# Sample-token side work in pairs: scores, values and state products of two samples issued together

## Chip, cores and metric

The kernel runs on one core of a Trainium2 chip. The metric is the device time of one launch in microseconds (us); lower is better. Before the change three runs gave 1600.12, 1600.78 and 1602.69 us; their median, 1600.78 us, is the time to compare with.

## What is computed

A decoder trunk of two layers runs one step for a prompt of 256 tokens and for 8 samples of 4 tokens each; both share the weights, so 288 token columns go past every weight tile. A layer is a half-step feed-forward (SwiGLU), a mixer with three branches (causal pooling, a Mamba-2 scan, cross-attention into 256 memory tokens), and a second half-step feed-forward. Three parts of the mixer belong to the samples alone, because every sample has its own cache. In the reference they are these lines, with L = 4 tokens for each of 8 samples:

```python
# cross-attention: k and v are the sample's cached keys and values (256, 4 heads, 128)
s = einsum('blhd,bmhd->bhlm', q, k) * 128 ** -0.5
w = softmax(s, axis=-1)
y = einsum('bhlm,bmhd->blhd', w, v)
# scan: h0 is the sample's cached state (16 heads, 64, 128), for one chunk of 4 tokens
y_off  = einsum('tgn,ghpn->tghp', cm, h0) * exp(acum)
h_last = h0 * exp(acum[-1]) + einsum('sgn,sghp->ghpn', bm, xdt * to_end)
```

The new state `h_last` of every sample is an output, 512 KB each; the cached keys, values and states are inputs of 512 KB per sample and layer.

## The kernel before

**The stream.** All weights lie in one packed array of 128x128 float32 tiles, in the order in which TensorE needs them. `Stream` (line 107) brings them in slabs of 8 tiles (SyncE issues the load `raw`, 512 KB), splits each slab into a high part `whi` (ScalarE, line 139) and a low part `wlo` (VectorE, or GpSimd while `pool_share` is set, line 148), and `mm3` (line 282) then makes three products of 288 columns for each tile: 24 matmuls per slab.

**Ticks and steps.** When `take()` (line 152) reaches a new slab, it calls `tick(s)` (line 162): load slab s+5, split, then `step()`, then split slab s+3 (high) and s+2 (low). `step()` (line 168) goes through the list of side work that is under way, in the order in which it was started, and runs one stage of each, that is, the Python generator up to its next `yield`. An item started with `delay` d sits out d steps first. So the place of a side instruction is fixed by the step in which its stage runs and by its item's place in the list; each engine runs its own instructions strictly in that program order. `W.finish()` runs the rest of an item at once.

**The mixer's steps.** `mixer()` (line 564) goes through groups of products: the query group `q` (4 slabs), 16 groups `xbc` (one slab each), 4 groups `u`, 8 groups `z`, then gates `g0`, `g2`, `g1` interleaved with the branch products `b0`, `b2`, `b1`, then `o`. During `xbc` every group starts a `conv` (line 587: VectorE and ScalarE work on 315 columns) and the low parts are made by GpSimd. "q-step n" is below the n-th step after the start of the `q` group, "u-step n" the n-th after the start of the first `u` group (u-step 0 is q-step 20).

**Side work of the samples.** For a sample b:
- `scores(b)` (line 1015) is started with delay 3 + b of the `q` group. It loads `kb`, and three steps later issues 4 matmuls of 32 output columns each (8 instructions in the trace, since a float32 product takes two) into the bank `ps_s`.
- `values(b)` (line 1039) has delay 17 + b: load `vb`, three steps later 8 matmuls (16 instructions) into `ps_av`. `load_prompt_kv` (line 1064) takes two buffers of the same pool at q-step 24.
- `sample_state(b)` (line 781) is started with delay 8 + 2b of the `u` group. Stage 0 loads the state `hb`; stage 1 lets GpSimd make `bm`, the sample's masked copy of B; stage 2 issues the `ps_yo` products (8 instructions of 32 columns), lets GpSimd multiply `hb` by its decay, and issues 4 `ps_up` matmuls that read `bm`; stage 3 lets VectorE add `ps_up` to `hb` (two instructions); stage 4 stores `hb`. Sample 7 also ends the sum `ps_yo` (its copy `ysb`, two transposes, `yoff`).

`sample_y` (line 902) and `group_norm` (line 915) come behind with delays 28 and 30 and end before the `b1` products. The caches share the pool `k4` of 5 buffers; `bm` lives in the pool `t2` of 5; PSUM has 7 rotating banks and one (`sum_bank`) for the sums `ps_s`, `ps_av`, `ps_yo` in turn. `pool_mix` (line 955) of a `u` group has GpSimd sums `pw`, then VectorE's `pd`, then the product `ps_pool`.

Of the kernel before, what the change touches and what calls it, by code (L numbers as in the profile page):

```python
# [20 lines left out]
NM = 256  # L21
# [23 lines left out]
def group_order(tiles, cuts):  # L45
    """Weight tiles (tile, k) of a group of products: all tiles up to each cut of k in turn."""
    for a, b in zip((0,) + cuts[:-1], cuts):
        for t in tiles:
            for k in range(a, b):
                yield t, k  # L50
# [56 lines left out]
class Stream:  # L107
    """Runs the packed weight tiles past TensorE, each split into two float32r parts.

    Every SLAB tiles make a tick: the split of a later slab is issued, then one stage  # L110
    of every piece of side work that is under way."""

# [8 lines left out]
    def parts(self, n):  # L121
        """The first slab comes in two halves, so that the products can begin."""
        k = 2 if n == 0 else 1
        return [slice(j * SLAB * P // k, (j + 1) * SLAB * P // k) for j in range(k)]
# [64 lines left out]
def trunk_kernel(ctx, tc, wpack, xT, memT, vecs, consts, wdt, wpool, hpool, hconv, h0T, kT, vC,  # L189
# [9 lines left out]
    ep = ctx.enter_context(tc.tile_pool(name="ep", bufs=2))  # L199
    t2 = ctx.enter_context(tc.tile_pool(name="t2", bufs=5))  # L200
    sp = ctx.enter_context(tc.tile_pool(name="sp", bufs=1))
# [7 lines left out]
    def tmp(name, cols=T, parts=P, dt=F32):  # L209
        return tp.tile([P, 384], dt, tag="t", name=name)[:parts, :cols]  # L210

# [9 lines left out]
    def blocks(name):  # L221
        """Two tiles of zeros for block_fill()."""
        us = [unit(f"{name}{j}") for j in range(2)]
        for u in us:
            G.memset(u, 0.0)
        return us

    def block_fill(us, srcs, copy):
        """Block b of 32 columns, of each of the four slices, gets the slice's samples with all but sample b zero."""
        for u, src in zip(us, srcs):  # L230
            copy(u.rearrange("p a (b s) -> p a b s", b=DB)[:, :, :, 0:DL], src.rearrange("p a (b t) -> p a b t", b=DB))
# [58 lines left out]
    def products(tiles, cuts, xs):  # L290
        """One PSUM bank per tile: W[:, cols].T @ x."""
        ps = [bank("ps") for _ in tiles]
        for j, k in group_order(range(len(tiles)), cuts):
            mm3(ps[j][:, :T], W.take(), chunk(xs[0], k), chunk(xs[1], k), k == 0, k == cuts[-1] - 1)
        return ps
# [9 lines left out]
    def rstd_cols(accs, starts, width, name):  # L305
        """1 / sqrt(mean + eps) of the column sums of accs, tokens on partitions: [128, len(accs) * len(starts)]."""
        n = len(accs) * len(starts)
        ps = bank("ps_" + name)
        for a, acc in enumerate(accs):
            for j, s in enumerate(starts):  # L310
                k = a * len(starts) + j
                mm(ps[:, k:k + 1], acc[:, s:s + P], ones[:, 0:1])
        v = sp.tile([P, 12], F32, tag="rs_v", name="rs_v", bufs=2)[:, :n]
        ts(v, ps[:, :n], 1.0 / width, ALU.mult, EPS, ALU.add)
        r = sp.tile([P, 12], F32, tag="rs_r", name="rs_r", bufs=2)[:, :n]
        act(r, v, AF.Sqrt)
        V.reciprocal(out=r, in_=r)
        stt(v, v, -0.5, r, ALU.mult, ALU.mult)
        tt(v, v, r, ALU.mult)
        stt(r, v, 1.5, r, ALU.add, ALU.mult)  # L320
        return r

    def rstd_rows(r, t, sums, width):
        """r = 1 / sqrt(sums / width + eps), elementwise; stages."""
        yield
# [10 lines left out]
    def spread(r):  # L336
        """out[p, t] = r of token t, for every partition p; r holds tokens 0.., 128.., 160.. by column."""
        ps = bank("ps_spread")
# [5 lines left out]
    class Norm:  # L344
        """Collects sum(x^2) chunk by chunk and splits x * gain for the products."""

# [22 lines left out]
    class Final:  # L369
        """The last norm: x * gain in place, then its scale and the output."""  # L370

# [38 lines left out]

# [1 line left out]
    mem = [unit(f"mem{j}") for j in range(KC // 2)]  # L412
# [112 lines left out]

# [1 line left out]
    def ffn(i, which, cur, nxt):  # L527
# [34 lines left out]

# [1 line left out]
    def mixer(i, cur, nxt):  # L564
# [65 lines left out]
        def dt_work(ps_dt):  # L630
# [18 lines left out]
            yield  # L649
            # log1p(e) = 2 atanh(e / (2 + e))  # L650
            ts(s, e, 2.0, ALU.add)
# [11 lines left out]
            yield  # L663
            # cumulative sums, heads on partitions and tokens on partitions; sums to the end of the group
            ph = bank("ps_nac")
# [115 lines left out]
        def sample_state(b):  # L781
            hb = k4.tile([P, D], F32, tag="k4", name="hb")
            nc.sync.dma_start(out=hb, in_=h0T[i, b])
            yield
            bm = wide("bm", 96, 512, F32R)
            tt(bm, Bst.bitcast(F32), con[:96, K_BM + b:K_BM + b + 1].to_broadcast([96, 512]), ALU.mult, G)
            yield
            if b == 0:
                yo.append(sum_bank("ps_yo"))
            for g in range(4):  # L790
                mm(yo[0][TS * g:TS * g + TS, :256], block(cm, g, b), hb[:, g * 256:(g + 1) * 256], b == 0, b == DB - 1)
            h3 = hb.rearrange("p (h d) -> p h d", h=H)
            tt(h3, h3, Ee[:, b, :].unsqueeze(2).to_broadcast([P, H, 64]), ALU.mult, G)
            pu = [bank("ps_up0"), bank("ps_up1")]
            for g in range(4):
                mm(pu[g // 2][:, (g % 2) * 256:(g % 2 + 1) * 256], bm[:, g * P:(g + 1) * P],
                   xst[g // 2][:, (g % 2) * 256:(g % 2 + 1) * 256])
            yield
            if b == DB - 1:
                ysb = wide("ysb", P, 256)  # L800
                act(ysb, yo[0][:, :256], AF.Copy)
            for q in range(2):
                tt(hb[:, q * 512:(q + 1) * 512], hb[:, q * 512:(q + 1) * 512], pu[q], ALU.add)
            yield
            nc.sync.dma_start(out=o_ssm_s[i, b], in_=hb)
            if b == DB - 1:
                pt = bank("ps_yot")
# [6 lines left out]
        def heads4(g):  # L814
            """Four heads of the prompt's scan: two pairs of heads, one group of B and C."""
            hs = slice(4 * g, 4 * g + 4)
# [169 lines left out]
        def softmax(ps, n):  # L986
            """Rows of ps [128, n, 256] (scores) to weights; stages."""
            sc = P ** -0.5
# [26 lines left out]
        def scores(b):  # L1015
            kb = k4.tile([P, 4, NM], F32, tag="k4", name="kb")
            nc.sync.dma_start(out=kb, in_=kT[i, b])
            yield
            yield
            yield  # L1020
            if b == 0:
                sc_.append(sum_bank("ps_s"))
            for h in range(4):
                mm(sc_[0][TS * h:TS * h + TS, :NM], block(qm, h, b), kb[:, h, :], b == 0, b == DB - 1)

# [13 lines left out]
        def values(b):  # L1039
            vb = k4.tile([P, 2, 512], F32, tag="k4", name="vb")  # L1040
            nc.sync.dma_start(out=vb, in_=vC[i, b])
            yield
            yield
            yield
            if b == 0:
                av.append(sum_bank("ps_av"))
            for m in range(2):
                for h in range(4):
                    mm(av[0][TS * h:TS * h + TS, :P], block(pm[m], h, b), vb[:, m, h * P:(h + 1) * P],
                       b == 0 and m == 0, b == DB - 1 and m == 1)  # L1050
            if b == DB - 1:
                yield
# [88 lines left out]
        for kind, cs, tiles, cuts in mixer_groups():  # L1141
            c = cs[0]
            # side work that this group's products need, or that can begin here
            if kind == "q":
                items["qm"] = W.start(q_blocks(), 2)
                items["sc"] = [W.start(scores(b), 3 + b) for b in range(DB)]
                items["sw"] = W.start(sample_weights(), 15)
                items["kv"] = W.start(load_prompt_kv(), 24)
                items["va"] = [W.start(values(b), 17 + b) for b in range(DB)]
                items["ph"] = [W.start(prompt_head(h), 27 + 5 * h // 2) for h in range(4)]  # L1150
                ym.extend(unit(f"ym{j}") for j in range(2))
            if kind == "u" and c == 0:
                W.pool_share = 0
                items["xss"] = W.start(xss_work(), 3)
                items["ss"] = [W.start(sample_state(b), 8 + 2 * b) for b in range(DB)]
                items["pairs"] = [W.start(heads4(g), 4 + 4 * g) for g in range(4)]
                items["yo"] = W.start(sample_y(), 28)
                items["gn"] = W.start(group_norm(), 30)
            if kind == "z" and c == 0:
# [182 lines left out]
```

## Time and profile before

| what | value |
|---|---|
| median of 3 runs | 1600.78 us (1600.12 to 1602.69) |
| span of the profiled execution, first to last instruction (the page gives no other time of it) | 1597.1 us |
| TensorE busy | 1558.0 us (98%), 11792 matmuls |
| VectorE / ScalarE / GpSimd busy | 1066.3 / 804.0 / 302.9 us |
| DMA moved | 278.00 MB, mean 174 GB/s |
| loads of `kb`, `vb`, `hb`; stores of `hb` | 16 each, 512 KB each |

PE is TensorE, DVE VectorE, ACT ScalarE, POOL GpSimd, SPq the queue of SyncE that issues all DMAs. Matmuls overlap in the array, so the trace shows the start of each; the cost of a batch is best read from the distance between starts. The page's chain of work follows what ended last backwards. [...]

### The profile page before, as it was taken

What the parts mean: (1) busy time and instruction counts of PE and PEld (TensorE: products, weight loads), DVE (VectorE), ACT (ScalarE), POOL (GpSimd) and SP (SyncE); (2) the same over time, 40 slices, a digit from 0 to 9 for tenths busy, and PEclk for the clock granted to TensorE, in tenths of its full rate; (3) what the DMA queues carried; (4) which work ended last, traced back from release to release, by engine and by line L of the source; (5) the groups of instructions that cost most, each with busy time, mean ns of one, the idle gap of its engine ahead of it and who ended that gap; (6) DMA issues with size and microseconds to landing.
All of it is one profiled execution on the core that took longest, in us unless ns stands there. A gap on an engine that the chain in (4) does not pass through costs nothing.

```text
span 1597.1 us, 29305 instructions
## 1 busy us (share of the span) xinstructions
PE 1558.0 (98%) x11792; PEld 1502.7 (94%) x11792; DVE 1066.3 (67%) x1598; ACT 804.0 (50%) x1231; POOL 302.9 (19%) x368
## 2 busy tenths in 40 slices
PE   7999999988999999999999999999999999999997
PEld 6899999887889999999999999988888999999997
DVE  6765645788777867656456665588778786766643
ACT  7444434465565546444445444456557454644442
POOL 3000001368233102000000000046823320200001
PEclk9999999999999999999999999999999999999999
DMA  6744444546465454444444444554655545444452
GB/s 244 230 167 166 164 165 171 196 147 233 168 212 193 147 173 167 162 165 166 165 166 160 171 161 169 178 185 151 238 170 188 203 159 169 158 168 167 159 171 70
DMA packets 81287, 278.00 MB, mean 174 GB/s; under 512 B 9088, under 2 KB 14336, under 8 KB 81152
## 3 DMA queue, kind: packets, MB, share of 16 engines
q1 hardware_dynamic: 81152, 276.14, 50.2%
q8 instruction: 92, 1.51, 0.4%
q14 instruction: 43, 0.35, 0.1%
HBM read 262.39 MB, written 13.71 MB: 173 GB/s over the span
## 4 chain that ended last, share of the span: by engine, by line
PE 87%; DVE 8%; ACT 2%; DMA 1%; POOL 1%; issue 1%; SPq 0%; DVEq 0%; ACTq 0%; POOLq 0%
PE ps L249 61%; PE pd L249 18%; DVE cacc L246 4%; PE ps_y L249 2%; PE ps_v L249 1%; PE ps_k L249 1%; ACT L252 1%; DMA raw<-wpack 1%; PE ps_up L249 1%; DVE wlo L148 1%; DVE cbuf L237 1%; ACT cacc L252 1%; PE ps_yo L249 1%; ACT whi L139 1%; PE ps_sp L249 0%
## 5 line engine op out<-in xcount | busy, mean ns | idle before, releaser
L148 DVE TENSOR_TENSOR wlo<-raw,whi 128x1024 fp32r<-128x1024 f32 (+1 forms) x409 | 517.8, 1267 | 266.8 <-ACT hidh L252 99.9
L139 ACT ACTIVATE whi<-raw 128x1024 fp32r<-128x1024 f32 (+1 forms) x441 | 463.7, 1054 | 329.3 <-PE ps L249 153.2
L249 PE MATMUL ps<-n1h,whi 128*128 128x288 f32 x896 | 274.4, 306 | 5.4 <-DVE Bst L237 5.4
L249 PE MATMUL ps<-n1h,wlo 128*128 128x288 f32 x896 | 266.9, 298 | 4.8 <-POOL wlo L148 4.8
L249 PE MATMUL ps<-n1l,whi 128*128 128x288 f32 x896 | 266.3, 297 | 0.0
L249 PE MATMUL ps<-n2h,whi 128*128 128x288 f32 x704 | 208.8, 297 | 0.0
L249 PE MATMUL ps<-n0h,whi 128*128 128x288 f32 x704 | 208.6, 296 | 0.0
L249 PE MATMUL pd<-hidh,whi 128*128 128x288 f32 x704 | 208.4, 296 | 0.0
L249 PE MATMUL ps<-n0l,whi 128*128 128x288 f32 x704 | 207.7, 295 | 0.0
L249 PE MATMUL pd<-hidl,whi 128*128 128x288 f32 x704 | 207.7, 295 | 0.0
L249 PE MATMUL ps<-n2l,whi 128*128 128x288 f32 x704 | 207.7, 295 | 0.0
L249 PE MATMUL ps<-n2h,wlo 128*128 128x288 f32 x704 | 207.0, 294 | 0.0
L249 PE MATMUL ps<-n0h,wlo 128*128 128x288 f32 x704 | 207.0, 294 | 0.0
L249 PE MATMUL pd<-hidh,wlo 128*128 128x288 f32 x704 | 207.0, 294 | 0.0
L237 POOL TENSOR_TENSOR acc<-acc,sqr 128x288 f32<-128x288 f32 x42 | 44.7, 1064 | 786.9 <-ACT sqr L252 785.9
L249 PEld LDWEIGHTS ps<-n1h,whi 128*128 128x128 f32 x896 | 170.3, 190 | 16.1 <-DVE Bst L237 5.8
L249 PEld LDWEIGHTS ps<-n1h,wlo 128*128 128x128 f32 x896 | 170.4, 190 | 7.3 <-POOL wlo L148 6.9
L249 PEld LDWEIGHTS ps<-n1l,whi 128*128 128x128 f32 x896 | 170.5, 190 | 0.7
L249 PEld LDWEIGHTS ps<-n0h,wlo 128*128 128x128 f32 x704 | 132.6, 188 | 0.0
L249 PEld LDWEIGHTS pd<-hidh,wlo 128*128 128x128 f32 x704 | 132.6, 188 | 0.0
L249 PEld LDWEIGHTS ps<-n2h,wlo 128*128 128x128 f32 x704 | 132.6, 188 | 0.0
L249 PEld LDWEIGHTS ps<-n2l,whi 128*128 128x128 f32 x704 | 132.1, 188 | 0.1
(297 smaller groups left out, 2877.5 us busy)
## 6 DMA issues: line engine op xcount, KB each, us to landing
raw<-wpack SPq DMA_DIRECT2D x439, 512.0 KB, 3.3
kb<-kT SPq DMA_DIRECT2D x16, 512.0 KB, 5.1
vb<-vC SPq DMA_DIRECT2D x16, 512.0 KB, 4.6
hb<-h0T SPq DMA_DIRECT2D x16, 512.0 KB, 5.8
o_ssm_s<-hb SPq DMA_DIRECT2D x16, 512.0 KB, 5.0
x<-xT SPq DMA_DIRECT2D x4, 288.0 KB, 4.1
o_y<-x SPq DMA_DIRECT2D x8, 144.0 KB, 1.8
mem<-memT SPq DMA_DIRECT2D x4, 256.0 KB, 4.6
```

The lines of the kernel that those rows point to most:

```text
L139: nc.scalar.activation(out=hi[:, a], in_=self.loaded[self.n_hi][:, a], func=AF.Copy)
L148: eng.tensor_tensor(out=lo[:, a], in0=raw[:, a], in1=self.his[n][:, a].bitcast(F32), op=ALU.subtract)
L237: (eng or V).tensor_tensor(out=out, in0=a, in1=b, op=op)
L246: V.scalar_tensor_tensor(out=out, in0=a, scalar=s, in1=b, op0=op0, op1=op1)
L249: PE.matmul(out, lhsT=lhsT, rhs=rhs, start=start, stop=stop)
L252: A.activation(out=out, in_=a, func=func, **kw)
```

## The change

Scores, values and states are handled for samples b and b+1 by one item. The pair's loads are issued in two successive steps. `scores` and `values` then issue the products of both samples in one stage. `sample_state` makes the mask of b, issues the `ps_yo` products of both samples in one stage with the `ps_up` products of b, and makes the mask of b+1 behind the first decay; the `ps_up` products of b+1 come one step later. The delays are 6 + 5p for pair p, and `sample_y` and `group_norm` start one step later. The pool `t2` gets a sixth buffer, and the buffers of `tp` go from 384 to 320 columns. The other edits blank comments.

```diff
-    t2 = ctx.enter_context(tc.tile_pool(name="t2", bufs=5))
+    t2 = ctx.enter_context(tc.tile_pool(name="t2", bufs=6))
-        return tp.tile([P, 384], dt, tag="t", name=name)[:parts, :cols]
+        return tp.tile([P, 320], dt, tag="t", name=name)[:parts, :cols]
...
         def sample_state(b):
+            def masked(c):
+                bm = wide("bm", 96, 512, F32R)
+                tt(bm, Bst.bitcast(F32), con[:96, K_BM + c:K_BM + c + 1].to_broadcast([96, 512]), ALU.mult, G)
+                return bm
+            hbs = []
+            for c in (b, b + 1):
+                hbs.append(k4.tile([P, D], F32, tag="k4", name="hb"))
+                nc.sync.dma_start(out=hbs[-1], in_=h0T[i, c])
+                yield
+            bm = masked(b)
             yield
             if b == 0:
                 yo.append(sum_bank("ps_yo"))
+            for c, hb in zip((b, b + 1), hbs):
+                for g in range(4):
+                    mm(yo[0][TS * g:TS * g + TS, :256], block(cm, g, c), hb[:, g * 256:(g + 1) * 256], c == 0, c == DB - 1)
+            for c, hb in zip((b, b + 1), hbs):
+                h3 = hb.rearrange("p (h d) -> p h d", h=H)
+                tt(h3, h3, Ee[:, c, :].unsqueeze(2).to_broadcast([P, H, 64]), ALU.mult, G)
+                pu = [bank("ps_up0"), bank("ps_up1")]
+                for g in range(4):
+                    mm(pu[g // 2][:, (g % 2) * 256:(g % 2 + 1) * 256], bm[:, g * P:(g + 1) * P],
+                       xst[g // 2][:, (g % 2) * 256:(g % 2 + 1) * 256])
+                if c == b:
+                    bm = masked(c + 1)
+                yield
+                if c == DB - 1:
+                    ysb = wide("ysb", P, 256)
+                    act(ysb, yo[0][:, :256], AF.Copy)
+                if c > b:
+                    nc.sync.dma_start(out=o_ssm_s[i, b], in_=hbs[0])
+                for q in range(2):
+                    tt(hb[:, q * 512:(q + 1) * 512], hb[:, q * 512:(q + 1) * 512], pu[q], ALU.add)
+            yield
+            nc.sync.dma_start(out=o_ssm_s[i, b + 1], in_=hbs[1])
+            if b == DB - 2:
...
         def scores(b):
-            kb = k4.tile([P, 4, NM], F32, tag="k4", name="kb")
-            nc.sync.dma_start(out=kb, in_=kT[i, b])
-            yield
+            kbs = []
+            for c in (b, b + 1):
+                kbs.append(k4.tile([P, 4, NM], F32, tag="k4", name="kb"))
+                nc.sync.dma_start(out=kbs[-1], in_=kT[i, c])
+                yield
             yield
             yield
...
+            for c, kb in zip((b, b + 1), kbs):
+                for h in range(4):
+                    mm(sc_[0][TS * h:TS * h + TS, :NM], block(qm, h, c), kb[:, h, :], c == 0, c == DB - 1)
...
-                items["sc"] = [W.start(scores(b), 3 + b) for b in range(DB)]
+                items["sc"] = [W.start(scores(b), 3 + b) for b in range(0, DB, 2)]
-                items["va"] = [W.start(values(b), 17 + b) for b in range(DB)]
+                items["va"] = [W.start(values(b), 17 + b) for b in range(0, DB, 2)]
-                items["ss"] = [W.start(sample_state(b), 8 + 2 * b) for b in range(DB)]
+                items["ss"] = [W.start(sample_state(2 * p), 6 + 5 * p) for p in range(DB // 2)]
-                items["yo"] = W.start(sample_y(), 28)
-                items["gn"] = W.start(group_norm(), 30)
+                items["yo"] = W.start(sample_y(), 29)
+                items["gn"] = W.start(group_norm(), 31)
```

`values` changes as `scores` does.

## Rows read from the trace of the kernel before

**Rows 1.** The page's chain that ended last, shares of the span by engine.

```profile
PE 87%; DVE 8%; ACT 2%; DMA 1%; POOL 1%; issue 1%; SPq 0%; DVEq 0%; ACTq 0%; POOLq 0%
```

**Rows 2.** Waits of TensorE, whole span: us in total, times, longest.

```profile
PE ps_pool L249 <- DVE pd L237: 5.4, 2, 2.7
PE ps L249 <- DVE Bst L237: 5.4, 2, 2.7
PE ps L249 <- POOL wlo L148: 4.8, 8, 2.0
...
PE ps_gn L249 <- POOL gacc L237: 1.4, 2, 0.7
```

**Rows 3.** Busy time in three stretches: length, engines (instructions), clock, DMA share, GB/s.

```profile
288.00:370.30 82.30, 75.56 (x592) 66.42 (x590) 67.45 (x125) 47.52 (x85) 50.60 (x82) 1.00 0.47 165
1049.00:1131.00 82.00, 77.90 (x591) 69.00 (x589) 67.83 (x124) 47.44 (x85) 50.90 (x82) 0.96 0.48 168
399.00:493.00 94.00, 94.00 (x768) 82.93 (x766) 70.38 (x114) 55.50 (x113) 26.20 (x17) 1.00 0.56 190
```

**Rows 4.** The chain in order of time, layer 0: start us, us, what.

```profile
370.32 3.19 PE ps L249 x22
...
486.11 6.39 PE ps L249 x48
```

**Rows 5.** Timeline of TensorE at two batches of scores: start us, us, instruction.

```profile
301.12 0.29 PE L249 MATMUL ps<-n1h,wlo 128*128 128x288 f32 x1
301.35 0.64 PE L249 MATMUL ps_s<-kb,qm 128*32 128x256 f32 x8
...
302.15 0.29 PE L249 MATMUL ps<-n1l,whi 128*128 128x288 f32 x1
...
305.30 0.64 PE L249 MATMUL ps_s<-kb,qm 128*32 128x256 f32 x8
305.76 0.76 PE L249 MATMUL ps_nac<-con,dt 128*16 128x128 f32 x6
```

**Rows 6.** Timeline of TensorE at one sample's state products.

```profile
484.57 0.29 PE L249 MATMUL ps<-n1h,wlo 128*128 128x288 f32 x1
...
485.36 0.74 PE L249 MATMUL ps_up<-xst,bm 96*128 96x256 f32 x4
485.94 0.30 PE L249 MATMUL ps<-n1h,whi 128*128 128x288 f32 x1
```

**Rows 7.** Timeline of TensorE at the wait for pd, layer 0.

```profile
392.48 0.65 PE L249 MATMUL ps_av<-vb,pm 128*32 128x128 f32 x16
395.84 1.30 PE L249 MATMUL ps_pool<-pd,wp 128*128 128x288 f32 x2 [2.71 <-DVE pd L237]
...
400.98 0.64 PE L249 MATMUL ps_av<-vb,pm 128*32 128x128 f32 x16
```

**Rows 8.** Timelines of VectorE and GpSimd before that wait.

```profile
390.26 0.85 DVE L237 TENSOR_TENSOR xst<-xsw,xst 32x512 fp32r<-32x512 f32 x1 [5.37 <-ACT xst L252]
...
388.53 2.04 POOL L237 TENSOR_TENSOR xsw<-xss,wt 32x512 f32<-32x512 f32 x2
```

**Rows 9.** Busy time in two stretches behind TensorE waits, columns as in rows 3.

```profile
395.80:399.00 3.20, 3.16 (x12) 2.91 (x13) 3.20 (x5) 1.57 (x7) 2.86 (x2) 0.56 0.07 17
...
1116.00:1122.00 6.00, 5.84 (x24) 5.84 (x25) 5.16 (x9) 2.85 (x6) 4.07 (x9) 0.50 0.43 162
```

**Rows 10.** GpSimd's instructions on bm and hb: count, ns minimum/median/maximum, first and last start.

```profile
L237 POOL TENSOR_TENSOR bm<-Bst,con x16: 1035/1038/2021, 396.6 to 1248.8; 96x512 fp32r<-96x512 f32 x16
...
L237 POOL TENSOR_TENSOR hb<-hb,Ee x16: 1902/2115/2783, 419.5 to 1254.1; 128x1024 f32<-128x1024 f32 x16
```

**Rows 11.** Timelines of VectorE and TensorE in u-step 9.

```profile
409.73 0.51 DVE L246 SCALAR_TENSOR_TENSOR ypl<-ps_pool,vec,yph 128x288 fp32r<-128x288 f32 x1
...
413.20 0.30 PE L249 MATMUL ps_y<-Ms,xss 32*64 32x32 f32 x4
```

**Rows 12.** SyncE's queue at the load of sample 7's values, q-step 24.

```profile
382.85 0.33 SPq L1041 DMA_DIRECT2D vb<-vC  x1
```

More of the change, by code (lines that the diff above doesn't have):

```diff
@@ L781, in sample_state @@
         def sample_state(b):
-            hb = k4.tile([P, D], F32, tag="k4", name="hb")
-            nc.sync.dma_start(out=hb, in_=h0T[i, b])
-            yield
-            bm = wide("bm", 96, 512, F32R)
-            tt(bm, Bst.bitcast(F32), con[:96, K_BM + b:K_BM + b + 1].to_broadcast([96, 512]), ALU.mult, G)
+            def masked(c):
[8 more added lines that the diff above has]
+            bm = masked(b)
             yield
@@ L789, in sample_state @@
                 yo.append(sum_bank("ps_yo"))
[L790 to L797, printed above, removed]
-            yield
[L799 to L806, printed above, removed]
+            for c, hb in zip((b, b + 1), hbs):
[18 more added lines that the diff above has]
+                    tt(hb[:, q * 512:(q + 1) * 512], hb[:, q * 512:(q + 1) * 512], pu[q], ALU.add)
+            yield
+            nc.sync.dma_start(out=o_ssm_s[i, b + 1], in_=hbs[1])
+            if b == DB - 2:
                 pt = bank("ps_yot")
@@ L1015, in scores @@
         def scores(b):
-            kb = k4.tile([P, 4, NM], F32, tag="k4", name="kb")
-            nc.sync.dma_start(out=kb, in_=kT[i, b])
-            yield
+            kbs = []
[3 more added lines that the diff above has]
+                yield
             yield
@@ L1022, in scores @@
                 sc_.append(sum_bank("ps_s"))
-            for h in range(4):
-                mm(sc_[0][TS * h:TS * h + TS, :NM], block(qm, h, b), kb[:, h, :], b == 0, b == DB - 1)
+            for c, kb in zip((b, b + 1), kbs):
+                for h in range(4):
+                    mm(sc_[0][TS * h:TS * h + TS, :NM], block(qm, h, c), kb[:, h, :], c == 0, c == DB - 1)
         def sample_weights():
@@ L1039, in values @@
         def values(b):
-            vb = k4.tile([P, 2, 512], F32, tag="k4", name="vb")
-            nc.sync.dma_start(out=vb, in_=vC[i, b])
-            yield
+            vbs = []
+            for c in (b, b + 1):
+                vbs.append(k4.tile([P, 2, 512], F32, tag="k4", name="vb"))
+                nc.sync.dma_start(out=vbs[-1], in_=vC[i, c])
+                yield
             yield
@@ L1046, in values @@
                 av.append(sum_bank("ps_av"))
[L1047 to L1051, printed above, removed]
+            for c, vb in zip((b, b + 1), vbs):
+                for m in range(2):
+                    for h in range(4):
+                        mm(av[0][TS * h:TS * h + TS, :P], block(pm[m], h, c), vb[:, m, h * P:(h + 1) * P],
+                           c == 0 and m == 0, c == DB - 1 and m == 1)
+            if b == DB - 2:
                 yield
```

## The prediction

> **What bounds the kernel now.** I read the chain of waits first: TensorE makes 87% of it [rows 1]. So only what lengthens or shortens TensorE's way counts, and the second view is TensorE's own list of waits. It is short: 5.4 us on `pd`, 5.4 on `Bst`, 4.8 on low parts made by GpSimd, 1.4 on `gacc`, the same in both layers [rows 2]. The reader is to see in it that TensorE is almost never kept waiting, and that three of the four places lie inside the mixer, where the change works. The third view is busy time by stretch. From 399 to 493 us, where the states are done, TensorE is busy in all of 94.00 us: a microsecond taken from it there is a microsecond gained. In the `conv` stretch, where the scores lie, it is otherwise: layer 0 takes 82.30 us with 75.56 us of TensorE at clock 1.00, layer 1 takes 82.00 us with 77.90 us of it at clock 0.96 [rows 3]. TensorE needed 2.3 us more in layer 1 and the stretch was no longer. So this stretch is set by VectorE, ScalarE and GpSimd working in line, and TensorE has some 4 us to give away in it. It ends for TensorE at 370.32 us, when a low part made by GpSimd is there [rows 4]. Fourth, between 370 and 396 us, TensorE runs into the 2.71 us wait for `pd` [rows 7]; VectorE is late with it since it sat 5.37 us until ScalarE's `xst`, which follows GpSimd's `xsw` (388.53 to 390.57 us) [rows 8]. That wait, too, ends by other engines' work.
>
> **What a merged batch saves.** Stream matmuls start every 6.39 / 48 = 0.133 us [rows 4]. One batch of scores moves the stream from 301.12 to 302.15, two starts further, so it costs 1.03 - 0.27 = 0.76 us. Eight such instructions, followed at once by other small matmuls, take 305.76 - 305.30 = 0.46 us [rows 5]. A second sample directly behind the first should cost 0.46 instead of 0.76 us: 0.30 saved. Bounds: nothing saved (0.76), or 0.30. I take 0.30, since the row is of the same matmuls.
> [...]
>
> **Scores.** 4 pairs per layer, 0.30 us each: TensorE is 1.2 us earlier per layer, inside the `conv` stretch. The loads stay one per step, in the steps of before; VectorE, ScalarE and GpSimd get nothing new. I count 0: the cover is the wait for those engines, which grows by what TensorE saves. Without it the gain would be 8 x 0.30 = 2.4 us.
>
> **Values.** Products of samples 0 to 7 came in q-steps 20 to 27; now pairs come in 21, 23, 25 and 27. Samples 0 and 1 fall before the wait that ends at 370.32. Samples 2 to 6 lay before the `pd` wait (sample 6 at 392.48), sample 7 behind it (400.98) [rows 7]. Now 2 to 5 lie before it, in two batches, and 6 and 7 behind it. Before the wait TensorE saves 2 x 0.30 + 0.76 = 1.4 us, and the wait grows from 2.7 to about 4.1 us. Behind it sample 6 is new: +0.46 us per layer, +0.9 in both. Bounds: -2.4 us (nothing hidden) to +1.5 (second sample at full price).
> The buffers: in q-step 24 `vb4`, `vb5`, `vb6`, `kp` and `vp` hold all five of `k4`, and `vb7` now has to wait for the products of q-step 25, which before released `vb4` a step earlier. SyncE issued it at 382.85 [rows 12]; it now stands, with the weight loads queued behind it, at most until 392.48, where q-step 26 began its batch. `vb7` is needed some 8 us later, and the slabs queued behind are for four to five steps further, 13 us or more of stream. I count 0; if that cover goes, the excess delay of a slab is paid by TensorE.
>
> **States.** One sample costs 485.94 - 484.57 - 0.133 = 1.24 us, of which its `ps_up` takes 485.94 - 485.36 = 0.58 [rows 6]. A pair now costs 1.24 + 0.46 for the second `ps_yo`, and `ps_up` of b+1 alone in the next step. For that the trace has no row; from below 4 x 256/288 x 0.133 = 0.47 us, from above 0.58. I take 0.50, nearer to the lower end, as `ps_up` no longer follows small tiles. 2.20 instead of 2.48 us: 0.28 saved, times 8 pairs = 2.2 us (1.6 to 2.5 by these ends). This is the stretch where TensorE never waits, so it counts in full.
> What is moved there: b's state is loaded three steps before its use, b+1's two, as before. Stores wait for VectorE's additions one step earlier in both kernels. The additions, decays and masks are as many as before, and b's are issued in the same distance from its products; b+1's decay starts without a wait for TensorE. In u-step 9 the pair's first two `ps_up` banks come where, by program order, eight other tiles want seven banks, so TensorE waits until VectorE has read those of that step. The last of them ended at 410.24, and TensorE's own work of u-step 9 comes to `ps_y` at 413.20 [rows 11]: about 3 us of cover. `sample_y` and `group_norm` go one step back together, and the wait of 0.7 us per layer on `gacc` [rows 2] should stay; I give it 0.5 us either way. The pools `t2` and `tp` change no instruction.
>
> **Sum.** States -2.2, values +0.9, scores 0: -1.3 us, so 1595.8 against the span of 1597.1. The median of the runs is 3.7 us above that span, and the change touches nothing outside it; on the median the forecast is 1600.78 - 1.3 = 1599.5 us. Its own range is 1598.0 to 1601.5. No change within 0.2% (3.2 us: 1597.6 to 1604.0) is about what can be told apart here.
>
> **Rivals.**
> 1. Everything counts: the other engines are not the bound, and scores and values gain too. 16 x 0.30 + 8 x 0.28 = 7.0 us, 1593.8. For it: TensorE has 87% of the chain. Against it: the two `conv` stretches of equal length. 13%.
> 2. Slower: TensorE waits for the mask of b+1. GpSimd makes it behind b's decay. In two of four pairs nothing else stands between, and TensorE is back after 0.46 + 0.58 + 24 x 0.133 = 4.24 us, counted from the end of b's `ps_yo`. GpSimd needs 2.12 + 1.04 = 3.2 us at the medians, and 2.78 + 2.02 = 4.8 at the longest [rows 10]; if its decay also starts only behind the second sample's products, 5.3. Above 4.24 it decides. The longest would cost 0.56 to 1.02 us, 8 times: 4.5 to 8.2, less the 1.3: 1604.0 to 1607.7. Against it: the medians leave 1 us. 10%.
> [...]
> 3. The clock. Behind the `pd` wait TensorE ran 3.2 us at 0.56, which loses 1.4 us; behind the `Bst` wait of layer 1 six at 0.50, which loses 3.0 [rows 9]. With 4.1 us of idling the low stretch may last as long as the latter: +1.6 per layer, 1602.7 (14%). It may also miss the wait, as it did behind the same `Bst` wait in layer 0 (clock 1.00 in rows 3): -1.4 per layer, 1596.7 (6%).
> 4. The change doesn't do what it says: the second sample is as dear as the first. States 0, values 2 x 0.76 = +1.5: 1602.3. Only if the 0.46 us owes itself to the particular matmuls that follow there. 6%.
>
> **How the numbers follow.** The forecast has 47%, the rivals 49, 4 are left for stalls not seen. Faster by over 0.2%: rival 1, the second half of rival 3 and a little more, 0.21. Slower: rival 2 and a little of the longer clock drop, 0.12. The rest, 0.67, lies within 0.2%. The range that leaves out most of rivals 1 and 2 is 1595.0 to 1603.5.
>
> **What would show it.** Right: batches of 16 `ps_s` and `ps_yo` instructions in about 1.0 us; `ps_up` of b+1 alone in about 0.5; the `pd` wait near 4.1 us in both layers; more waiting on GpSimd's low parts or `Bst` (1.6 us per layer) in stretches of the same 82 us; the state stretch shorter by about 1.1 us per layer. Wrong: a `conv` stretch shorter by over 0.5 us (rival 1), a wait of `ps_up` on `bm` (rival 2), or a long stretch at clock 0.50 behind 396 us (rival 3).

## The result and the profile after

The changed kernel takes 1610.08 us (median of 4 runs, 1609.0 to 1610.97); the kernel before took 1600.72 us beside it. The ratio is 1.0054, 95% interval 1.004 to 1.0069: slower by 9.4 us, where 1.3 us faster was forecast. The span of the profiled execution is 1608.9 us.

The page's chain by engine, to be read against [rows 1]: TensorE has 81% instead of 87%, and VectorE and GpSimd have five points more of it together.

```profile
PE 81%; DVE 11%; POOL 3%; ACT 3%; issue 1%; DMA 0%; SPq 0%; DVEq 0%; ACTq 0%; POOLq 0%
```

The waits of TensorE in the kernel after, whole span (us in total, times, longest), answering to [rows 2]:

```profile
PE ps_pool L249 <- DVE pd L237: 12.0, 2, 6.0
PE ps L249 <- POOL wlo L148: 6.0, 8, 2.0
...
PE ps L249 <- DVE hb L237: 1.8, 2, 0.9
...
PE ps_gn L249 <- POOL gacc L237: 0.8, 2, 0.4
PE ps_y L249 <- DVE ym L1112: 0.5, 2, 0.3
PE ps L249 <- ACT st L252: 0.5, 2, 0.2
```

Two things are new. The wait for `pd` has grown from 2.7 to 6.0 us per layer, where 4.1 was forecast. And there are waits for `hb`, `ym` and `st`, that is, for VectorE in the state stretch (ScalarE's `st`, started at 427.62, waited for VectorE's `xs`, which ended at 427.59), where the kernel before had none. The merged products of the scores came out as counted. TensorE's timeline after, at one pair of scores:

```profile
302.99 0.29 PE L249 MATMUL ps<-n1h,wlo 128*128 128x288 f32 x1
303.22 1.07 PE L249 MATMUL ps_s<-kb,qm 128*32 128x256 f32 x16
304.22 0.40 PE L249 MATMUL ps<-n1h,whi 128*128 128x288 f32 x1
304.45 0.29 PE L249 MATMUL ps<-n1l,whi 128*128 128x288 f32 x1
```

Read as in [rows 5], two stream starts further, the pair costs 304.45 - 302.99 - 0.27 = 1.19 us, where 0.76 + 0.46 was forecast and two single batches cost 1.52. So it was not the merged products that lost the time.

**A measure for one layer.** The two profiles already differ in their first loads: the last weight load of `ps_k` starts at 51.6 us before and at 54.2 after, ahead of anything that the change touches. So I compare layer 0 from the first weight load of `ps_dt` to that of the product that reads `ysh` (`b1`). It takes 287.8 to 544.9 us before and 290.4 to 552.0 after: 257.1 and 261.6 us, so +4.5 us, twice that for two layers 9.0 of the 9.4 us measured.

| kernel | layer 0, us | time, us | ratio to the kernel before, 95% |
|---|---|---|---|
| before | 257.1 | 1600.52 | 1 |
| after | 261.6 | 1610.08 | 1.004 to 1.0069 |
| sixth buffer alone | 260.4 | 1606.66 | 1.0024 to 1.0049 |
| change, mask in its own pool | 258.8 | 1603.55 | 1.0012 to 1.003 |
| change, softmax on ScalarE | 259.6 | 1604.42 | 1.0015 to 1.0036 |
| change, both edits | 256.5 | 1598.41 | 0.998 to 0.9997 |
| before, softmax on ScalarE | 257.6 | 1601.14 | 0.9992 to 1.001 |
| own pool, softmax in the other form | 260.1 | 1607.4 | 1.0029 to 1.0054 |
| both edits, values unpaired | 255.9 | 1597.18 | 0.9965 to 0.9984 |
| both edits, state pairs only | 256.0 | 1597.79 | 0.9973 to 0.9991 |
| both edits, exponentials in PSUM | 256.5 | 1600.33 | 0.9987 to 1.0005 |

(The time of before is that of the shared runs of the first two groups of experiments; it was 1600.72 beside the changed kernel and 1600.92 beside the last one.)

### The profile page after: what moved, and what is told of

It is laid out like the page before. It is cut to its first block, busy times and chain, and to the rows that moved or that the text cites. A ratio compares the mean times of both kernels' runs of the same rounds, so it can differ in the third digit from the quotient of the medians.

```text
span 1608.9 us, 29300 instructions
## 1 busy us (share of the span) xinstructions
PE 1560.2 (97%) x11792; PEld 1511.0 (94%) x11792; DVE 1070.4 (67%) x1598; ACT 804.1 (50%) x1231; POOL 302.0 (19%) x368
## 4 chain that ended last, share of the span: by engine, by line
PE 81%; DVE 11%; POOL 3%; ACT 3%; issue 1%; DMA 0%; SPq 0%; DVEq 0%; ACTq 0%; POOLq 0%
PE ps L249 57%; PE pd L249 18%; DVE cacc L246 5%; PE ps_y L249 1%; POOL pw L237 1%; DVE wlo L148 1%; PE ps_k L249 1%; DVE pr L241 1%; PE ps_v L249 1%; DVE cbuf L237 1%; ACT L252 1%; ACT cacc L252 1%; DMA raw<-wpack 0%; DVE z L237 0%; ACT whi L139 0%
## 5 line engine op out<-in xcount | busy, mean ns | idle before, releaser
L148 DVE TENSOR_TENSOR wlo<-raw,whi 128x1024 fp32r<-128x1024 f32 (+1 forms) x409 | 512.5, 1255 | 266.1 <-ACT hidh L252 102.5
## 6 DMA issues: line engine op xcount, KB each, us to landing
mem<-memT SPq DMA_DIRECT2D x4, 256.0 KB, 4.9
```

What stands on the lines that cost most here:

```text
L148: eng.tensor_tensor(out=lo[:, a], in0=raw[:, a], in1=self.his[n][:, a].bitcast(F32), op=ALU.subtract)
```

## The first place: VectorE waits for a buffer

Timeline of the kernel after ahead of the wait for `pd`, first VectorE, then GpSimd, then TensorE (the brackets give the idle time before an instruction and what ended it); it answers to [rows 7, 8]:

```profile
394.22 0.84 DVE L237 TENSOR_TENSOR xst<-xsw,xst 32x512 fp32r<-32x512 f32 x1 [0.46 <-ACT xst L252]
396.80 0.69 DVE L237 TENSOR_TENSOR xd<-ps_x,dtt 128x512 f32<-128x512 f32 x1 [1.74 <-POOL pw L237]
...
399.58 0.89 DVE L237 TENSOR_TENSOR pd<-pf,ub 128x7 f32<-128x7 f32 x1
...
394.59 3.30 POOL L237 TENSOR_TENSOR pw<-pw 128x420 f32<-128x420 f32 x3
...
399.39 1.06 POOL L237 TENSOR_TENSOR bm<-Bst,con 96x512 fp32r<-96x512 f32 x1
...
400.62 1.30 PE L249 MATMUL ps_pool<-pd,wp 128*128 128x288 f32 x2 [6.02 <-DVE pd L237]
```

`xd` doesn't read `pw`. It waits for GpSimd because it is written into the buffer that a `pw` tile held. In the programs as built, the pool `t2` doesn't go round in turn; a tile gets a buffer that the bookkeeping holds for free. With five buffers, the layer's first `xd` lands where the first `xsw` was, last read by VectorE itself. With six it lands where the second of the four sums `pw` of the last `u` group was, which GpSimd still has to read for the third. The kernel before has no idle time ahead of that `xd`; VectorE's timeline there:

```profile
391.57 0.84 DVE L237 TENSOR_TENSOR xst<-xsw,xst 32x512 fp32r<-32x512 f32 x1 [0.46 <-ACT xst L252]
392.44 0.69 DVE L237 TENSOR_TENSOR xd<-ps_x,dtt 128x512 f32<-128x512 f32 x1
...
395.50 0.19 DVE L237 TENSOR_TENSOR pd<-pf,ub 128x7 f32<-128x7 f32 x1
```

And since `pd` stands behind `xd` on VectorE, TensorE waits for it.

From the start of that second `xst` to the end of the `pd` that TensorE waits for, VectorE took 4.12 us before and takes 6.25 us now: 1.74 for the buffer, 0.70 since the last `pd` now falls beside GpSimd's `bm` (0.89 us instead of 0.19), less 0.24 for a quicker piece.

Behind the wait the clock is low for longer. Busy time in stretches of 4 us from the end of the wait in layer 0 (the number behind POOL's is the TensorE clock granted, 1.00 being full speed), first the kernel before, then the one after:

```profile
395.84:399.84 4.00, 4.00 (x19) 3.71 (x20) 3.96 (x10) 2.37 (x10) 2.82 (x2) 0.65 0.23 61
399.84:403.84 4.00, 4.00 (x39) 3.43 (x38) 4.00 (x7) 3.69 (x8) 0.00 (x0) 1.00 0.81 249
```

```profile
400.62:404.62 4.00, 4.00 (x15) 3.71 (x16) 3.96 (x10) 2.01 (x7) 0.00 (x0) 0.50 0.40 122
404.62:408.62 4.00, 4.00 (x49) 3.56 (x49) 4.00 (x6) 2.85 (x5) 0.00 (x0) 0.89 0.93 345
```

Behind 2.7 us of idling TensorE lost 4 x 0.35 = 1.4 us here to the lower clock (0.65); behind 6.0 us it lost 4 x 0.50 + 4 x 0.11 = 2.4 (0.50 and 0.89). Of the 3.3 us by which the wait has grown, 2.1 are the sixth buffer's; the experiments below set them apart from the 1.2 that the values' new order brings.

## The second place: VectorE stands still beside GpSimd

Timeline of the kernel after in the state stretch, VectorE, then GpSimd, then TensorE:

```profile
420.24 0.15 DVE L1012 RECIPROCAL sm<-sm 128x2 f32<-128x2 f32 x1
420.43 2.76 DVE L241 TENSOR_SCALAR pr<-pr,sm 128x256 f32<-128x256 f32 x2
423.11 0.68 DVE L1005 TENSOR_REDUCE mx<-ps_sp 128x2 f32<-128x512 f32 x1
423.82 2.16 DVE L241 TENSOR_SCALAR mx<-mx 128x2 f32<-128x2 f32 x1
425.89 1.27 DVE L237 TENSOR_TENSOR hb<-hb,ps_up 128x512 f32<-128x512 f32 x2
...
450.36 4.77 DVE L241 TENSOR_SCALAR pr<-pr,sm 128x256 f32<-128x256 f32 x2
...
420.08 1.90 POOL L237 TENSOR_TENSOR hb<-hb,Ee 128x1024 f32<-128x1024 f32 x1 [19.63 <-DVE wlo L148]
421.94 1.09 POOL L237 TENSOR_TENSOR bm<-Bst,con 96x512 fp32r<-96x512 f32 x1
422.99 1.09 POOL L237 TENSOR_TENSOR xw<-xd,wt 128x512 f32<-128x512 f32 x1
424.05 1.90 POOL L237 TENSOR_TENSOR hb<-hb,Ee 128x1024 f32<-128x1024 f32 x1
...
426.71 1.01 PE L249 MATMUL ps_up<-xst,bm 96*128 96x256 f32 x4
427.95 0.40 PE L249 MATMUL ps<-n1h,whi 128*128 128x288 f32 x1 [0.23 <-ACT st L252]
...
456.62 0.40 PE L249 MATMUL ps<-yph,whi 128*128 128x288 f32 x1 [0.92 <-DVE hb L237]
```

`mx` multiplies two numbers per partition by a constant, in 0.17 us elsewhere. Here it takes 2.16 us and ends with GpSimd's `hb` (425.98 and 425.95 us). The two multiplications of `pr` take 0.61 us where GpSimd is idle and 4.77 us where it works without a pause. The additions of `ps_up` to `hb` stand behind them on VectorE and free the PSUM banks, so TensorE waits (0.92 us ahead of 456.62).

The kernel before had the same instructions, with gaps. Its timeline there, VectorE, then GpSimd:

```profile
426.83 0.62 DVE L241 TENSOR_SCALAR pr<-pr,sm 128x256 f32<-128x256 f32 x2
...
443.40 2.91 DVE L241 TENSOR_SCALAR pr<-pr,sm 128x256 f32<-128x256 f32 x2
...
419.45 2.71 POOL L237 TENSOR_TENSOR hb<-hb,Ee 128x1024 f32<-128x1024 f32 x1 [3.85 <-PE ps_yo L249]
422.12 1.03 POOL L237 TENSOR_TENSOR bm<-Bst,con 96x512 fp32r<-96x512 f32 x1
428.38 2.32 POOL L237 TENSOR_TENSOR hb<-hb,Ee 128x1024 f32<-128x1024 f32 x1 [5.22 <-PE ps_yo L249]
```

One decay and one mask, 3.7 us, then a pause of 5.2. The pair puts two decays, a mask and at times `xw` in one run: 5.9 us from 420.08 to 425.95.

## The experiments

**The sixth buffer alone** in the kernel before (with the smaller `tp` buffers that go with it).

```diff
-    t2 = ctx.enter_context(tc.tile_pool(name="t2", bufs=5))
+    t2 = ctx.enter_context(tc.tile_pool(name="t2", bufs=6))
-        return tp.tile([P, 384], dt, tag="t", name=name)[:parts, :cols]
+        return tp.tile([P, 320], dt, tag="t", name=name)[:parts, :cols]
```

> The kernel before with the two pool edits alone: the pool of wide tiles has six buffers instead of five, and the small tiles are 320 columns instead of 384; no pairs. Theory A (the sixth buffer gives xd of the first four heads a buffer that a pooling sum still holds, so VectorE waits 1.7 us for GpSimd and pd comes 2.1 us later): 2 x 2.1 us slower than before, about 1605 us, with a pd wait of some 4.5 us per layer in place of 2.7. Rival B (the later pd comes from the pairs, not from the pool): the time of before, 1600.7 us, pd wait 2.7.

Measured: 1606.66 us, +6.1. All instructions of VectorE stand in the same order as before; one waits. Its timeline, VectorE, then TensorE:

```profile
396.24 0.69 DVE L237 TENSOR_TENSOR xd<-ps_x,dtt 128x512 f32<-128x512 f32 x1 [1.74 <-POOL pw L237]
...
400.06 1.30 PE L249 MATMUL ps_pool<-pd,wp 128*128 128x288 f32 x2 [4.82 <-DVE pd L237]
```

The same 1.74 us, with no pair of samples anywhere; the wait of TensorE grows by 2.1 us (2.71 to 4.82). In the two stretches of 4 us behind it the granted clock is 0.50 and 0.84 in layer 0, a loss of 4 x 0.50 + 4 x 0.16 = 2.6 us instead of 1.4. Together that is 3.3 us, as much as layer 0 got longer (260.4 instead of 257.1).

**The change with the mask in a pool of its own**, `t2` back at five buffers.

```diff
-    t2 = ctx.enter_context(tc.tile_pool(name="t2", bufs=6))
+    t2 = ctx.enter_context(tc.tile_pool(name="t2", bufs=5))
+    bmp = ctx.enter_context(tc.tile_pool(name="bmp", bufs=1))
-                bm = wide("bm", 96, 512, F32R)
+                bm = bmp.tile([P, 512], F32R, tag="bm", name="bm")[:96, :]
```

> The changed kernel with the masks bm in a pool of their own (one buffer) and the pool of wide tiles back at five buffers; the pairs stay. Theory A: VectorE's wait for GpSimd ahead of xd goes, the pd wait falls from 6.0 to about 4.1 us per layer: 2 x 2.1 us faster than the changed kernel, 1605.8 us. Rival B: as the changed kernel, 1610 us, pd wait 6.0.

Measured: 1603.55 us, 6.5 less than the change, where 4.2 was expected. `xd` no longer waits, and the wait for `pd` is 3.87 us per layer; the waits for `hb` (0.9 per layer) stay. The smaller `tp` buffers stay too, so it is the sixth buffer and not they that made `xd` wait.

**The change with the softmax's two multiplications on ScalarE.**

```diff
-            ts(mx[:, :n], mx[:, :n], -sc, ALU.mult)
+            act(mx[:, :n], mx[:, :n], AF.Copy, scale=-sc)
-                ts(pr[:, a * 256:(a + 1) * 256], pr[:, a * 256:(a + 1) * 256], sm[:, a:a + 1], ALU.mult)
+                act(pr[:, a * 256:(a + 1) * 256], pr[:, a * 256:(a + 1) * 256], AF.Copy, scale=sm[:, a:a + 1])
```

> The changed kernel with the softmax's two multiplications by a scalar (mx and pr) moved from VectorE to ScalarE. Theory C (GpSimd's decay, mask and decay without a pause keep VectorE's scalar multiplications from going on, 2.8 and 4.8 us instead of 0.6 to 1.4, so that VectorE's additions, PSUM banks and low parts are late): the waits of TensorE on hb go, the stretch from the pd wait to the b1 products is about 2.3 us per layer shorter, about 1605.5 us. Rival D (the stretch is longer by the clock after the longer pd wait and by what the pairs add to TensorE alone): no faster than the changed kernel, 1610 us, or slower by ScalarE's extra work.

Measured: 1604.42 us, 5.7 less than the change. The wait for `pd` stays at 6.02 us. From its end to the `b1` products layer 0 now takes 149.0 us instead of 151.4, 2.4 less where 2.3 was expected. The waits for `hb`, `ym` and `st`, all gone, were 1.4 us of that. The list counts only time in which TensorE is idle; a batch that stalls inside adds to it (from the start of `ps_up` to the stream's return it was 427.95 - 426.71 = 1.24 us, and is 0.48 here).

**Both edits.**

> Both edits of the two runs before in the changed kernel: masks in their own pool, softmax multiplications on ScalarE. Theories A and C together: 1610.1 - 4.2 - 4.6 = about 1601 us, what the pairs themselves are worth being then at most a microsecond or two. If only one of them holds, about 1606 us; if neither, 1610 us.

Measured: 1598.41 us, 11.7 less than the change and 2.1 less than the kernel before (0.998 to 0.9997). About 1601 had been expected, with prices of 4.2 and 4.6 us that were both too low. The two costs add up: the buffer is worth 6.5 and 6.0 us, without and with the softmax edit, the softmax edit 5.7 and 5.1. TensorE's timeline with both edits, at one pair of states:

```profile
442.58 1.07 PE L250 MATMUL ps_yo<-hb,cm 128*32 128x256 f32 x16
443.58 0.74 PE L250 MATMUL ps_up<-xst,bm 96*128 96x256 f32 x4
444.16 0.30 PE L250 MATMUL ps<-n1h,whi 128*128 128x288 f32 x1
```

The pair takes 1.58 us from its first start to the stream's. Its second `ps_up`, alone among stream products, is shown best in the pair before it; with it stand two lines of VectorE and GpSimd for the last section:

```profile
420.74 0.64 PE L250 MATMUL ps_up<-xst,bm 96*128 96x256 f32 x4
421.21 0.30 PE L250 MATMUL ps<-n1h,whi 128*128 128x288 f32 x1
...
421.31 1.21 DVE L148 TENSOR_TENSOR wlo<-raw,whi 128x1024 fp32r<-128x1024 f32 x1
...
421.52 1.90 POOL L238 TENSOR_TENSOR bm<-Bst,con 96x512 fp32r<-96x512 f32 x1 [1.35 <-PE ps_up L250]
```

It costs 0.47 us. Together 2.05 us, and some 0.1 more for the step into the batch, where 2.20 was counted.

**Is the softmax edit a gain by itself?** It was put into the kernel before.

> The kernel before, with the softmax's two multiplications by one number per partition moved from VectorE to ScalarE, and nothing else. Theory (they are slow only where GpSimd works beside them without a pause, which the kernel before hardly shows: 0.62 to 2.91 us for the pair, and no wait of TensorE behind it): within 1.5 us of the kernel before, 1599.5 to 1602, and no gain. Rival (the move is a gain by itself, whatever the change did): the 5.1 us that it was worth between the mask's own pool alone and both edits together, so about 1595.5; then the both-edits kernel owes its lead over before to the move and not to the pairs.

Measured: 1601.14 us, ratio 0.9992 to 1.001: no gain. (It shifts waits there: 2.7 us less for `Bst` over both layers, 3.0 more for ScalarE's `pr` of the samples.) So the edit takes away a cost that the change brought, and the lead over the kernel before is the pairs'.

**The other form.** The change with the mask's own pool, and the multiplications on VectorE as products of two tensors.

```diff
+    nsc = cp.tile([P, 1], F32, name="nsc")
+    G.memset(nsc, -P ** -0.5)
...
-            ts(mx[:, :n], mx[:, :n], -sc, ALU.mult)
+            tt(mx[:, :n], mx[:, :n], nsc.to_broadcast([P, n]), ALU.mult)
-                ts(pr[:, a * 256:(a + 1) * 256], pr[:, a * 256:(a + 1) * 256], sm[:, a:a + 1], ALU.mult)
+                tt(pr[:, a * 256:(a + 1) * 256], pr[:, a * 256:(a + 1) * 256], sm[:, a:a + 1].to_broadcast([P, 256]), ALU.mult)
```

> The change with the mask in its own pool (t2 at five buffers), and the softmax's two multiplications still on VectorE, but written as products of two tensors (a broadcast operand in place of a number per partition). Theory (it is the form with one number per partition that stands still beside GpSimd's work): these instructions take under 1 us each whatever GpSimd does beside them, TensorE's waits for hb go, and the time is that of the both-edits kernel, 1598 to 1600. Rival 1 (VectorE simply has too much to do there, and any instruction beside GpSimd is slow): as the mask's own pool alone, 1603 to 1604. Rival 2 (two-tensor instructions are slow beside GpSimd as well, but less so): between, about 1601.

Measured: 1607.4 us, above all three expectations; the theory that the form with one number per partition is to blame has fallen. VectorE's timeline, then a line of GpSimd's:

```profile
344.23 2.28 DVE L238 TENSOR_TENSOR mx<-mx,nsc 128x1 f32<-128x1 f32 x1
...
421.16 2.15 DVE L238 TENSOR_TENSOR mx<-mx,nsc 128x2 f32<-128x2 f32 x1
...
447.69 5.03 DVE L238 TENSOR_TENSOR pr<-pr,sm 128x256 f32<-128x256 f32 x2
...
344.11 2.38 POOL L148 TENSOR_TENSOR wlo<-raw,whi 128x1024 fp32r<-128x1024 f32 x1
```

The two-tensor products stand still as long (5.03 and 2.15 us), and in one place they do where the other form didn't: `mx` of one number per partition takes 2.28 us beside GpSimd's `wlo` and ends with it (346.51 and 346.49 us), and took 0.15 us as a multiplication by a constant beside the same `wlo`. Behind it `cbm` is late, and TensorE waits 1.2 us per layer for it; the waits for `hb` grow by 0.7. Twice 1.9 is 3.8 us, and 1607.4 lies 3.85 above the mask's own pool alone.

Three kinds of instruction were not slowed beside GpSimd's work: `mx` from `ps_sp` (0.68 us) and the `hb` additions (1.29 for two beside `bm` in the kernel before, with one operand in PSUM), which read PSUM, and the reciprocal (0.15). That gave the new theory, tried last.

**Exponentials in PSUM.** Both edits, but the prompt's `pr` multiplied on VectorE again, from PSUM.

```diff
+            ex = ps if n == 2 else pr
...
-                act(pr[:, a * 256:(a + 1) * 256], ps[:, a * 256:(a + 1) * 256], AF.Exp, scale=sc, bias=mx[:, a:a + 1],
+                act(ex[:, a * 256:(a + 1) * 256], ps[:, a * 256:(a + 1) * 256], AF.Exp, scale=sc, bias=mx[:, a:a + 1],
...
-                act(pr[:, a * 256:(a + 1) * 256], pr[:, a * 256:(a + 1) * 256], AF.Copy, scale=sm[:, a:a + 1])
+                if n == 2:
+                    ts(pr[:, a * 256:(a + 1) * 256], ps[:, a * 256:(a + 1) * 256], sm[:, a:a + 1], ALU.mult)
+                else:
+                    act(pr[:, a * 256:(a + 1) * 256], pr[:, a * 256:(a + 1) * 256], AF.Copy, scale=sm[:, a:a + 1])
```

> The both-edits kernel, with the multiplication of the prompt's softmax weights back on VectorE, but reading its operand from PSUM: ScalarE leaves the exponentials in the scores' bank, and VectorE multiplies from there into SBUF. Same engine, same instruction with one number per partition, same place beside GpSimd's work; only the operand's memory differs from the mask's own pool alone, where the pair of multiplications took up to 4.8 us. Theory (what stands still beside GpSimd is a VectorE instruction whose tensors all lie in SBUF): the pairs take 0.6 to 1.1 us everywhere, no wait of TensorE for hb, and the time is within 2 us of the both-edits kernel, 1597 to 1600.5. Rival (any multiplication of VectorE there stands still, or VectorE has too much to do): pairs of 2.8 to 4.8 us again, waits for hb of about 0.9 us per layer, 1601 to 1603.5.

Measured: 1600.33 us, ratio 0.9987 to 1.0005. Layer 0 takes 256.5 us, as with both edits, and no wait for `hb` is left. (The median is 1.9 us above that with both edits; layer 0 does not show where.) VectorE's instruction (count, ns minimum, median and maximum) in that kernel:

```profile
L242 DVE TENSOR_SCALAR pr<-ps_sp,sm x16: 473/479/485, 417.5 to 1218.3; 128x256 f32<-128x256 f32 x16
```

All sixteen take 0.473 to 0.485 us, those beside GpSimd too. With the operand in SBUF, the same sixteen and two more took 0.35 to 2.99 us (with the mask in its own pool). So for these multiplications it is not VectorE's load that decides, but where the operand lies. One more pair is slow beside GpSimd in this kernel as with both edits, and has its operands in SBUF: two `E<-E,cbm`, 1.82 us elsewhere, take 3.31 beside GpSimd's second `hb`, but no wait of TensorE is put down to it.

Set side by side, two multiplications of `pr` beside GpSimd's work take 4.77 us by numbers and 5.03 us as products of two tensors, with their operands in SBUF, against 0.88 us from PSUM. The 0.70 us more of `pd` in the first place are one more case: it has two SBUF inputs and ends with GpSimd's `bm` (400.47 and 400.45 us). By what mechanism the two engines hold each other up, no run shows.

**Values unpaired, and then scores too.** The kernel with both edits, `values` as before the change; then `scores` too.

```diff
-                items["va"] = [W.start(values(b), 17 + b) for b in range(0, DB, 2)]
+                items["va"] = [W.start(values(b), 17 + b) for b in range(DB)]
...
-                items["sc"] = [W.start(scores(b), 3 + b) for b in range(0, DB, 2)]
+                items["sc"] = [W.start(scores(b), 3 + b) for b in range(DB)]
```

> The both-edits kernel (mask in its own pool, softmax multiplications on ScalarE) with the value products unpaired, as before the change; scores and states still go by pairs. Theory, the prediction's term: pairing the values costs 0.46 us per layer by the order of the stores plus what the longer wait adds, 0.9 to 2 us in two layers, so 1596.5 to 1597.7, and the wait for pd falls from 3.9 back to about 2.7 us. Rival (the merged batches of the values gain 0.3 us each and the wait is paid back later): 1598.4 or more.

> The both-edits kernel with values and scores unpaired, as before the change: only the state stretch goes by pairs. Theory, the prediction's term of zero for the scores: the same as without the value pairs, within 0.5 us. Rival (the score pairs' 0.3 us a batch, eight batches, count in full): 2.4 us slower than without the value pairs.

Measured: 1597.18 us without the value pairs and 1597.79 with the state pairs alone. TensorE's timeline without the value pairs:

```profile
393.13 0.65 PE L250 MATMUL ps_av<-vb,pm 128*32 128x128 f32 x16
396.45 0.72 PE L250 MATMUL ps_pool<-pd,wp 128*128 128x288 f32 x2 [2.67 <-DVE pd L238]
```

Sample 6 is ahead of the wait again, which is back at 2.67 us, and the time is 1.2 us lower: pairing the values costs (0.6 us of it in layer 0, though the intervals of the two ratios overlap a little: 0.998 to 0.9997 and 0.9965 to 0.9984). The score pairs are worth nothing that can be told: 255.9 and 256.0 us in layer 0, and the 0.6 us that the median rises without them is a quarter of the rival's 2.4, inside the intervals. The kernel without the value pairs has the lowest median of all, but is not set apart from the state pairs alone.

## Why the prediction was wrong

By its own steps; two of them failed, and they make up the whole miss: with the means of the two prices above, 6.3 + 5.4, less the 2.1 that the pairs are worth, gives 9.6 us; 9.4 was measured.

1. **"The pools `t2` and `tp` change no instruction."** This is the larger failure. The sentence is true, and the price of nothing drawn from it is not: 6.1 us alone, 6.0 to 6.5 within the change. I asked what the pool does to instructions and not what it does to who gets whose buffer. [rows 7, 8] showed how little slack there was: `pd` was already the last to come, and `xd` stands ahead of it on VectorE.
2. **States: "The additions, decays and masks are as many as before".** I counted GpSimd's instructions and not how close they now follow one another. The price is 5.1 to 5.7 us. Rival 2 had the place (GpSimd behind b's decay) and, by luck, nearly the time that this cost alone gives (1604.0 to 1607.7; 1603.55 with the mask in its own pool), but not the mechanism: TensorE never waits for `bm`; it is VectorE that stands still, with 4.77 us for two multiplications of `pr`. The signs stood in the trace of before and I did not read them: `pr` at 0.62 and at 2.91 us.
3. **"this is the stretch where TensorE never waits, so it counts in full"** held only with the softmax edit. There the state pairs alone give 1600.52 - 1597.79 = 2.7 us (1.4 to 4.3 by the interval), and 1601.14 - 1597.79 = 3.35 against the kernel before with the same softmax edit, where 2.2 was forecast. Each term (0.46 for a second sample, 0.50 for `ps_up` alone) was right to 0.03 us; the shorter wait for `gacc` is 0.6 more in two layers.
4. **Values +0.9**: right, as far as can be told. With both edits they cost 1.2 us, and the `pd` wait grows from 2.67 to 3.88 us (forecast: 2.7 to 4.1).
5. **Scores 0**: right: layer 0 is as long with them as without. From the first weight load of `ps_dt` to VectorE's first `ub` behind the `conv` stretch it is 87.5 us both with the score pairs (values unpaired) and with the state pairs alone. The rows below this list show that TensorE doesn't set this stretch; which of the other engines does was not tried. The sign came out smaller than forecast: 1.2 us more waiting on low parts in both layers together (6.0 instead of 4.8) and none more on `Bst`, where 1.6 per layer was given. TensorE's clock in the stretch was 0.96 instead of 1.00 in layer 0, which by these rows leaves it less to wait.
6. **The clock** (rival 3) was right in part: the low stretch is longer, by 1.0 us in layer 0, but behind a wait of 6.0 us. Behind 3.9 us, with both edits, it was nearly as before: 0.58 in the first 4 us and 1.00 in the next in layer 0, 0.64 and 0.93 in layer 1, a loss of 1.7 us in each. So the 1.6 us per layer more that the rival gave for 4.1 us of idling did not come.
7. The wait for `vb7`, u-step 9 and `gacc`: 0 was right for each; `gacc` fell from 0.7 to 0.4 us per layer, inside the 0.5 given.

For step 5, the stretch named there in two kernels without any pairs, first the one before, then the sixth buffer alone (columns as in [rows 3]):

```profile
287.80:374.90 87.10, 80.34 (x638) 70.83 (x637) 72.11 (x133) 50.11 (x90) 52.93 (x86) 1.00 0.49 171
```

```profile
289.80:377.00 87.20, 82.94 (x638) 73.90 (x637) 72.19 (x133) 50.09 (x90) 52.97 (x86) 0.96 0.47 170
```

At the lower clock TensorE was busy 2.6 us longer, and the stretch took only 0.1 more.

Of the pairs alone, then, -1.3 us was forecast and -2.1 measured (0.998 to 0.9997 of the kernel before). What was missed is what the change did to instructions that it does not touch.

One thing stays open: of the some 3 us per layer that the sixth buffer costs, the profiles show 2.1 as waiting; what the clock adds does not follow the length of the wait (in layer 1 the changed kernel lost 2.2 us to it behind 6.0 us of waiting, the sixth buffer alone 3.0 behind 4.8), and no run set it apart.

## What to carry to other kernels

Price a changed pool by asking, for the tiles next to every wait that is already on the critical path, whose buffer each now gets and which engine reads it last; an added buffer can add a wait (1.74 us of VectorE and 2.1 of TensorE per layer here). When work on GpSimd moves closer together, look in the trace of before for VectorE instructions on SBUF whose longest time is several times their shortest (`pr` here: 0.34 to 1.86 us), and see what stands behind them; moving them to ScalarE (5.1 to 5.7 us less), or the operand of the prompt's `pr` to PSUM with the others on ScalarE (0.88 instead of up to 4.77 us for two), took the cost away here. A merge that saves in one place shows up in the total only after both have been done.

## What was not expected of the hardware

- A VectorE multiplication of two numbers per partition took 2.16 us beside GpSimd and 0.17 us without; one number per partition took 0.15 us even beside GpSimd's `wlo`, but 2.28 us as a product of two SBUF tensors.
- GpSimd was slowed beside VectorE too: with both edits its mask took 1.90 us instead of 1.04 where VectorE's `wlo` (two SBUF inputs, 421.31 to 422.52 us) had started 0.2 us before it.
